# A hybrid SSD and attention layer: the fourth z block moved behind B, and a second step cut in slices

## The chip, the cores and the metric

The kernel runs on one core of a Trainium2 chip. The metric is the device time of one execution in microseconds (us), as the median of several executions. Before the change it is 838.3 us (three runs, 838.29 to 838.42).

## The reference

One layer over 256 tokens of width 2048, in float32. The input is normalised, goes through one wide projection whose columns belong to two groups, a state-space (SSD) scan and a causal attention without softmax, and both results go through an output projection:

```python
h = rmsnorm(x, norm_w)
proj = h @ w_in
z, xbc, dt_raw, q, k, v, g = jnp.split(proj, IN_SPLITS, axis=-1)
xbc = silu(causal_depthwise_conv(xbc, conv_w, conv_b))      # -> xs (2048), B (512), C (512)
y = ssd_chunked_scan(xs, softplus(dt_raw + dt_bias), -exp(a_log), bm, cm) + d_skip * xs
yg = y * silu(z);  y_ssd = group_rmsnorm(yg) * ssd_norm_w   # four groups of 512
y_sba = stick_breaking_attention(q, k, v) * silu(g)         # 16 heads of 128
out = rmsnorm(x + concat(y_ssd, y_sba) @ w_out, final_norm_w)
```

w_in is 2048 x 13344 and w_out 4096 x 2048; reading them is most of the traffic, and multiplying with them is most of the work.

## The kernel before

**Blocks and steps.** The projections are a list of blocks (L922 to L953), each of some columns of a weight. The blocks of z (z0 to z3, 512 columns), c1 (C's second half and dt), v and o have the kind "tok": the tokens are the rows of the result. Those of c0, b, x, q, k and g have the kind "feat", with 256 columns: the features are the rows. Order before: z0 to z3, c0, c1, b0, b1, the first half of q0, x0_0 to x3_1, the second half of q0, k0, v0, g0, then q, k, v, g of the attention groups 1 to 3, then o0 to o3. A block of z has 8 steps, each of two slices of 128 rows of the weight, and a block of "feat" has 4 steps of four slices.

**One step.** `load` (L192) fetches two steps' weights at once into one of four buffers (raw) by SyncE's queue. `cut` (L207) splits a step's weights into hi, a rounded copy by ScalarE (L222), and lo, the rest by VectorE (L225); activations are split in the same way (hT_hi, hT_lo). `product` (L240) then multiplies: for "tok" three matmuls of 512 columns for each slice and half of the tokens (L253 to L255), 12 in a step; for "feat" matmuls of 512 (L259) and of 256 columns (L262), 16 in a step. The cuts run two steps ahead of the products (`ahead=2`).

**The first block.** In z0, `run_blocks` (L279) writes the order out by hand. For each step s: `turn_x` (L387) transposes two slices of x on TensorE, `scale_x` (L398) scales each by norm_w and splits it (ScalarE, then VectorE), and `advance` calls `cut`. In step 0 this goes slice by slice, `scale_x` and then half of the cut; in the steps from 1 on both `scale_x` come first and then one cut over both slices. z0 also loads x, in eight parts between its weights (L200).

**The rows' scale.** hT is at first x * norm_w without the norm's factor 1/rms per token. z0 to z3 are multiplied with that, and the factor r_tok is applied when the result is taken out of PSUM (`fin_z`, L441, L445: a SiLU with `scale=r_tok`). `square_x`, `row_scale` and `row_scale_bc` work the factor out during z1. `scale_h` (L427), eight calls of one ScalarE and three VectorE operations, then multiplies hT by it in place: slice pair i after step i + 2 of z3, the last two in c0 (L924). All later blocks use the scaled hT.

**Side work.** Everything between the blocks (convolutions, the scan, the attention) sits in queues as small functions with a cost for VectorE and one for ScalarE. After each step `drain` (L145) takes functions from the queues, in the order of the queues, until a budget, 1.5 and 1.6 for most blocks, is used; a rest below zero is carried on. `lag` keeps a queue closed for so many steps after a function, `when` waits for a condition. `drain_all` (L166) empties all queues; `fin_proj` calls it at the end of g0 (L763), and then gives the scan's memory (pool ssd) to the attention's tiles.

**The scan.** After each x block `conv` (L465) runs; after a group's second block `ssd_group` (L620) queues: `back` (transposes and two VectorE operations of 512 columns for each half), `state_in` (L661, one VectorE operation), `decay` (eight exps, L654), `state` (L666, the product `ps_st`), `mat`, `yoff`, `yout` (L682, the products `ps_y`, then the gate with sz, L690, and squares), `scale` (a chain of small VectorE operations), `rescale` (L704) and `mix` twice (L708: transposes `ps_ms`, then L716 on ScalarE and L717 on VectorE). The small results in PSUM (`side_ps`, L70) share four buffers; a block's accumulators have their own two.

**The attention.** For each of a group's four heads `scores` (L780: `ps_z`, three sigmoids, four masks on GpSimd, a scan and products on VectorE), `weights_T` (L803: transposes `ps_w`) and `attend` (L813) are queued, staggered over the heads.

**The order on the engines.** Outside z0 it is not the written order: when the program is built, a planner with modelled durations places each instruction on its engine by its place in the program, with the cuts ahead, and lets later ones go first where an earlier one isn't ready by the model. The exps of group 0's `decay`, for instance, are called in x2 and run from 154.9 us on, in q0_0. On the chip each engine keeps to the order so made.

Of the kernel before, what the change touches and what calls it, by code (L numbers as in the profile page):

```python
# [12 lines left out]
AF = mybir.ActivationFunctionType  # L13
# [9 lines left out]
KIN = D_MODEL // P  # L23
# [29 lines left out]
def hybrid_kernel(ctx, tc, x, norm_w, w_in, conv_w, conv_b, dt_bias, a_log, d_skip,  # L53
                  ssd_norm_w, w_out, final_norm_w, out):
    nc = tc.nc
    ve, ac, te, gp = nc.vector, nc.scalar, nc.tensor, nc.gpsimd
# [13 lines left out]
    def side_ps(name):  # L70
        return ps_s.tile([P, 512], F32, tag="s", name=name)
# [70 lines left out]
    def push(q, cost, fn, lag=0, when=None):  # L142
        q.items.append((cost, lag, fn, when))
# [32 lines left out]
    def block(name, w, c0, n, nk, acts, kind, finish, budget, start=None, pool=None, trail=0):  # L176
        blocks.append(dict(name=name, w=w, c0=c0, n=n, nk=nk, acts=acts, kind=kind, finish=finish, budget=budget,
                           start=start, pool=pool, trail=trail))

    def chunks():  # L180
        for b in blocks:
            for kc in range(b["nk"] // KC[b["kind"]]):
                yield b, kc

    def steps():
        for b in blocks:
            for s in range(b["nk"] // KS[b["kind"]]):
                yield b, s

    raws, cuts, last_cut, after = {}, {}, [None], {}  # L190
# [88 lines left out]
    def run_blocks(ahead=2):  # L279
        todo_load, todo_cut = chunks(), steps()  # L280
        lead = {"load": 0, "cut": 0}
        done = 0

        def advance_load(want):
            while lead["load"] < want:
                c = next(todo_load, None)
                if c is None:
                    break
                load(*c)
                lead["load"] += 1  # L290

        def advance(n_cut, each=None):
            while lead["cut"] < n_cut:
                nxt = next(todo_cut, None)
                if nxt is None:
                    return
                b, s = nxt
                advance_load(lead["cut"] // 2 + 4)
                if s == 0 and b["start"] is not None:
                    b["start"]()  # L300
                with (tc.high_priority() if b is not blocks[0] else ExitStack()):
                    cut(b, s, each)
                lead["cut"] += 1


        with tc.manual_schedule(engines={te.engine, ac.engine, ve.engine}):
            b = blocks[0]
            acc = new_acc(b)
            advance_load(2)

            ac.copy(ysq[:, 0, 0:1], ones[:, 0:1])
            warm = side_ps("warm")

            def warm_up(n):
                for i in range(n):
                    te.matmul(warm[:, 0:P], lhsT=ident, rhs=ident, start=True, stop=True)
            warm_up(5)
            load_rows(nwT, nw_rows, KIN, "ps_nw")
            turn_x(0)
            warm_up(2)  # L320
            advance(1, each=scale_x)
            product(b, 0, acc, range(NB), (0,))
            for s in range(1, KIN // 2 + 1):
                if s < KIN // 2:
                    turn_x(s)
                    for i in range(2):
                        scale_x(2 * s + i)
                    advance(s + 1)
                product(b, s - 1, acc, range(NB), (1,) if s == 1 else None)
                done += 1  # L330
            load_params()
        b["finish"](acc)

        for b in blocks[1:]:
            name, trail = b["name"], b["trail"]
            ns = b["nk"] // KS[b["kind"]]
            acc = new_acc(b)
            for s in range(ns + trail):
                advance(done + 1 + ahead)
                if trail == 0:  # L340
                    product(b, s, acc, range(2))
                else:
                    if s < ns:
                        product(b, s, acc, (0,))
                        if s == ns - 1:
                            b["finish"](acc, 0)
                    if s == ns + trail - 1:
                        halves = [ps_mm.tile([P, 2, 512], F32, tag="mm", name=f"mm_{name}_1_{h}")[:, 0, :]
                                  for h in range(2)]
                        product_end(b, s - trail, 1, halves)  # L350
                    elif s >= trail:
                        product(b, s - trail, acc, (1,))
                if s < ns:
                    done += 1
                if (name, s) in after:
                    after[name, s]()
                drain(b["budget"])
            if trail == 0:
                b["finish"](acc)
            else:  # L360
                b["finish"]([acc[1]] + halves, 1)

    r_tok = const.tile([P, NB], F32, name="r_tok")
# [23 lines left out]
    def turn_x(s):  # L387

        q, h = divmod(s, 2)
        for j in range(2):  # L390
            k = 2 * s + j
            pt = side_ps(f"ps_x_{k}")
            for b in range(NB):
                te.transpose(out=pt[:, b * P:(b + 1) * P],
                             in_=xt[q][:, b, h * 256 + j * P:h * 256 + (j + 1) * P], identity=ident)
            xT[k] = pt[:, 0:SEQ]

    def scale_x(k):  # L398
        ac.activation(hT_hi[:, k, :], xT[k], AF.Copy, scale=nwT[:, k:k + 1])
        ve.scalar_tensor_tensor(out=hT_lo[:, k, :], in0=xT[k], scalar=nwT[:, k:k + 1],  # L400
                                in1=hT_hi[:, k, :].bitcast(F32), op0=ALU.mult, op1=ALU.subtract)
# [25 lines left out]
    def scale_h(s):  # L427

        ks = slice(2 * s, 2 * s + 2)
        hi, lo = hT_hi[:, ks, :], hT_lo[:, ks, :]  # L430
        t = ssd.tile([P, 2, SEQ], F32, tag="tmp", name=f"h_{s}", bufs=2)
        ve.tensor_tensor(out=t, in0=hi.bitcast(F32), in1=lo.bitcast(F32), op=ALU.add)
        ve.tensor_tensor(out=t, in0=t, in1=r_bc.unsqueeze(1).broadcast_to([P, 2, SEQ]), op=ALU.mult)
        ac.copy(hi, t)
        ve.tensor_tensor(out=lo, in0=t, in1=hi.bitcast(F32), op=ALU.subtract)


    sz = [mixp.tile([P, NB, GW], F32, tag="mix1", name=f"sz_{g}", bufs=4) for g in range(GROUPS)]
    main = queue()

    def fin_z(i):  # L441
        def f(acc):
            def evac():
                for t in range(NB):
                    ac.activation(sz[i][:, t, :], acc[t], AF.Silu, scale=r_tok[:, t:t + 1])  # L445
            if i > 0:
                evac()
                return
            for q in range(KIN // 4):
                for b in range(NB):  # L450
                    push(main, (0, 0.7), lambda q=q, b=b: square_x(q, b))
            push(main, (1.0, 0), row_scale, lag=1)
            push(main, (0.6, 0.7), row_scale_bc)
            push(main, (0, 1.1), evac, lag=8)
            push(main, (0.5, 0), turn_params)
        return f
# [142 lines left out]
    norm_q, scan_q, conv_q = queue(), queue(), queue()  # L599
    turned, summed, scanned, segs = set(), set(), set(), {}  # L600
# [19 lines left out]
    def ssd_group(g, w):  # L620
# [103 lines left out]
        if g == 0:  # L724
            push(scan_q, (0, 0), lambda: seg(0), when=lambda: g in turned)
            push(scan_q, (0, 0), lambda: seg(1), lag=3)
        push(scan_q, (0.6, 0), state_in, lag=1, when=lambda: g in turned)
        push(scan_q, (0, 2.4), lambda: decay(0))
        push(scan_q, (0, 0.6), state)
        push(scan_q, (1.2, 0), lambda: mat(0), lag=1)  # L730
# [188 lines left out]
            return mix_hi[k // 4][:, k % 4, :], mix_lo[k // 4][:, k % 4, :]  # L919
        return mix_a["hi"][:, k - KIN, :], mix_a["lo"][:, k - KIN, :]  # L920

    for i in range(4):  # L922
        block(f"z{i}", w_in, Z0 + i * 512, 512, KIN, h_acts, "tok", fin_z(i), (1.5, 1.6))
    for i in range(8):  # L924
        after[*(("z3", i + 2) if i < 6 else ("c0", i - 6))] = lambda i=i: scale_h(i)
    block("c0", w_in, C0, 256, KIN, h_acts, "feat", fin_c0, (1.5, 1.6))
    block("c1", w_in, C0 + 256, 256 + HEADS, KIN, h_acts, "tok", fin_c1, (0.7, 0.8))
    for h in range(2):
# [5 lines left out]
    def block_att(which, grp, halves=range(2)):  # L934
        c0 = {"q": Q0, "k": K0, "v": V0, "g": G0}[which] + grp * 512
        if which == "v":
            block(f"v{grp}", w_in, c0, 512, KIN, h_acts, "tok", fin_proj("v", grp), (1.5, 1.6))
            return
        for h in halves:
            block(f"{which}{grp}_{h}", w_in, c0 + h * 256, 256, KIN, h_acts, "feat", fin_proj(which, grp, h), (1.5, 1.6))  # L940


    block_att("q", 0, (0,))
    for g in range(GROUPS):
        block_x(g)
    block_att("q", 0, (1,))
    for grp in range(4):
        for which in "qkvg" if grp else "kvg":
            block_att(which, grp)
    for i in range(4):  # L950
        block(f"o{i}", w_out, i * 512, 512, 2 * KIN, m_acts, "tok", fin_last if i == 3 else fin_out(i), (1.5, 1.6),
# [32 lines left out]
```

## Time and profile before

| | |
|---|---|
| median of the runs | 838.3 us |
| profiled execution, its own time | 837.85 us |
| its span, from first to last instruction | 836.1 us |
| TensorE (PE) busy | 821.3 us, 98% |
| weight loads of TensorE (PEld), beside the matmuls | 701.2 us, 84% |
| VectorE (DVE) busy | 519.7 us, 62% |
| ScalarE (ACT) busy | 446.3 us, 53% |
| GpSimd (POOL) busy | 61.8 us, 7% |

The blocks lie in the span about like this: z0 from 6 to 33 us, z1 to 55, z2 to 77, z3 to 99, c0 and c1 to 123, b to 147, q0_0 to 158, x to 261, q0_1 to 276, k0 to 301, v0 to 327, g0 to 357, then the attention's groups 1 to 3 to about 650, and o to the end. A busy TensorE is not one at its peak, since the ends of matmuls are modelled and overlap the next one's start; from one start to the next a matmul of 512 columns takes about 0.23 us here.

### The profile page before, as it was taken

How to read it: one execution, taken by the hardware profiler on the slowest of the kernel's cores; microseconds unless marked ns; L12 is line 12 of the kernel's file. 1: busy time of each engine (PE TensorE's matmuls, PEld its weight loads, DVE VectorE, ACT ScalarE, POOL GpSimd, SP SyncE). 2: the span in 40 equal slices, each digit the busy share in tenths (PEclk: the TensorE clock that was granted, in tenths of full speed). 3: DMA queues.
4: the chain of work that ended last, by engine and by line, in shares of the span. 5: the costliest groups of instructions: out<-in, count | busy, mean ns of one | idle time of the engine just before them, and what ended most of it. 6: DMA issues, size and time to landing. Idle time of an engine off the chain costs nothing.

```text
span 836.1 us, 11189 instructions
## 1 busy us (share of the span) xinstructions
PE 821.3 (98%) x4345; PEld 701.2 (84%) x4345; DVE 519.7 (62%) x713; ACT 446.3 (53%) x670; POOL 61.8 (7%) x125
## 2 busy tenths in 40 slices
PE   8999999999999999999999999999999999999995
PEld 7888898888887888888888888888888888888884
DVE  5655968578798867667445754466545755455543
ACT  5754558865685747464444544455444444344433
POOL 0000000100100101013000400022000310000000
PEclk9999999999999999999999999999999999999999
DMA  9855476665556555554466546654565845555712
GB/s 311 280 180 192 136 231 201 207 197 169 190 160 211 172 182 177 151 151 152 153 201 201 152 150 201 196 165 150 194 184 179 343 151 186 184 188 198 252 51 102
DMA packets 114410, 155.29 MB, mean 186 GB/s; under 512 B 3212, under 2 KB 79140, under 8 KB 113972
## 3 DMA queue, kind: packets, MB, share of 16 engines
q1 hardware_dynamic: 112996, 149.29, 56.1%
q0 software_dynamic: 1328, 5.28, 1.7%
q8 instruction: 34, 0.56, 0.3%
q14 instruction: 20, 0.16, 0.1%
q10 hardware_dynamic: 32, 0.01, 0.0%
HBM read 152.43 MB, written 2.13 MB: 185 GB/s over the span
## 4 chain that ended last, share of the span: by engine, by line
PE 92%; DVE 3%; ACT 2%; issue 1%; POOL 0%; ACTq 0%; POOLq 0%
PE mm_k L259 7%; PE mm_g L259 7%; PE mm_x L259 7%; PE mm_o L254 7%; PE mm_o L253 7%; PE mm_o L255 7%; PE mm_q L259 5%; PE mm_k L262 4%; PE mm_g L262 4%; PE mm_z L254 4%; PE mm_v L253 3%; PE mm_v L255 3%; PE mm_v L254 3%; PE mm_z L253 3%; PE mm_x L262 3%; PE mm_z L255 3%
## 5 line engine op out<-in xcount | busy, mean ns | idle before, releaser
L225 DVE TENSOR_TENSOR lo_o<-raw_o,hi_o 128x1024 fp32r<-128x1024 f32 x64 | 78.1, 1224 | 74.1 <-ACT hi_o L222 74.1
L222 ACT CAST hi_o<-raw_o 128x1024 fp32r<-128x1024 f32 x64 | 67.1, 1053 | 93.5 <-PE mm_o L255 79.9
L259 PE MATMUL mm_q<-hT,hi_q 128*128 128x512 f32 x256 | 82.7, 402 | 0.0
L259 PE MATMUL mm_x<-hT,hi_x 128*128 128x512 f32 x256 | 81.8, 401 | 0.0
L259 PE MATMUL mm_k<-hT,hi_k 128*128 128x512 f32 x256 | 81.5, 400 | 0.0
L259 PE MATMUL mm_g<-hT,hi_g 128*128 128x512 f32 x256 | 81.0, 398 | 0.0
L225 DVE TENSOR_TENSOR lo_v<-raw_v,hi_v 128x1024 fp32r<-128x1024 f32 x32 | 39.2, 1224 | 41.4 <-ACT hi_v L222 41.4
L225 DVE TENSOR_TENSOR lo_g<-raw_g,hi_g 128x1024 fp32r<-128x1024 f32 x32 | 39.2, 1224 | 40.4 <-ACT hi_g L222 39.5
L222 ACT CAST hi_v<-raw_v 128x1024 fp32r<-128x1024 f32 x32 | 33.7, 1052 | 50.7 <-PE mm_v L255 31.6
L262 PEld LDWEIGHTS mm_k<-hT,lo_k 128*128 128x128 f32 x256 | 48.1, 188 | 11.4
L262 PEld LDWEIGHTS mm_x<-hT,lo_x 128*128 128x128 f32 x256 | 48.1, 188 | 11.4
L262 PEld LDWEIGHTS mm_g<-hT,lo_g 128*128 128x128 f32 x256 | 48.1, 188 | 11.3
L262 PEld LDWEIGHTS mm_q<-hT,lo_q 128*128 128x128 f32 x256 | 48.1, 188 | 11.2
L225 DVE TENSOR_TENSOR lo_q<-raw_q,hi_q 128x1024 fp32r<-128x1024 f32 x32 | 39.2, 1225 | 29.1 <-ACT hi_q L222 24.7
L222 ACT CAST hi_g<-raw_g 128x1024 fp32r<-128x1024 f32 x32 | 33.6, 1050 | 42.8 <-PE mm_g L259 27.8
L222 ACT CAST hi_q<-raw_q 128x1024 fp32r<-128x1024 f32 x32 | 33.5, 1048 | 42.3 <-PE mm_q L259 17.0
L225 DVE TENSOR_TENSOR lo_k<-raw_k,hi_k 128x1024 fp32r<-128x1024 f32 x32 | 39.2, 1226 | 24.7 <-ACT hi_k L222 23.7
L225 DVE TENSOR_TENSOR lo_z<-raw_z,hi_z 128x1024 fp32r<-128x1024 f32 (+1 forms) x33 | 39.2, 1191 | 22.8 <-ACT hi_z L222 22.7
L225 DVE TENSOR_TENSOR lo_x<-raw_x,hi_x 128x1024 fp32r<-128x1024 f32 x32 | 39.2, 1225 | 19.7 <-ACT hi_x L222 18.0
L253 PE MATMUL mm_z<-hi_z,hT 128*128 128x512 f32 x128 | 51.1, 399 | 0.0
L254 PE MATMUL mm_z<-lo_z,hT 128*128 128x512 f32 x128 | 50.2, 392 | 0.8 <-DVE lo_z L225 0.8
L262 PE MATMUL mm_q<-hT,lo_q 128*128 128x256 f32 x256 | 50.6, 279 | 0.0
(250 smaller groups left out, 1977.6 us busy)
## 6 DMA issues: line engine op xcount, KB each, us to landing
raw_o<-in_w_out_dram SPq DMA_DIRECT2D x32, 1024.0 KB, 5.2
raw_q<-in_w_in_dram SPq DMA_DIRECT2D x16, 1024.0 KB, 5.3
raw_x<-in_w_in_dram SPq DMA_DIRECT2D x16, 1024.0 KB, 5.4
raw_k<-in_w_in_dram SPq DMA_DIRECT2D x16, 1024.0 KB, 5.3
raw_v<-in_w_in_dram SPq DMA_DIRECT2D x16, 1024.0 KB, 5.0
raw_g<-in_w_in_dram SPq DMA_DIRECT2D x16, 1024.0 KB, 5.3
raw_z<-in_w_in_dram SPq DMA_DIRECT2D x12, 1024.0 KB, 5.0
raw_b<-in_w_in_dram SPq DMA_DIRECT2D x4, 1024.0 KB, 5.4
```

What stands on the lines that cost most here:

```text
L222: ins = ac.copy(hi[:, ks, :], src[:, ks, :])
L225: ve.tensor_tensor(out=lo[:, ks, :], in0=src[:, ks, :], in1=hi[:, ks, :].bitcast(F32), op=ALU.subtract)
L253: te.matmul(o, lhsT=ah[:, ts], rhs=hi[:, k2, :], start=first, stop=False)
L254: te.matmul(o, lhsT=ah[:, ts], rhs=lo[:, k2, :], start=False, stop=False)
L255: te.matmul(o, lhsT=al[:, ts], rhs=hi[:, k2, :], start=False, stop=last)
L259: te.matmul(acc[i], lhsT=hi[:, k2, i * P:(i + 1) * P], rhs=hT[:, k, :, :].rearrange("p a s -> p (a s)"), start=first, stop=False, skip_gro ...
L262: te.matmul(acc[i][:, 0:SEQ], lhsT=lo[:, k2, i * P:(i + 1) * P], rhs=hT_hi[:, k, :], start=False, stop=last, skip_group_check=True)
```

## The change

- In z0's step 1 the activations and weights are prepared slice by slice, as in step 0: `scale_x`, half of the cut, `scale_x`, the other half.
- The block z3 moves from behind z2 to behind b1. The first half of q0, which stood there, moves behind x3_1, so that q0 is now whole, right before k0.
- `scale_h` follows the steps of z2 instead of z3. So z3 is multiplied with the scaled hT, and its evacuation has no `scale=r_tok`.
- `state_in` gets a lag of 2 steps instead of 1.

```diff
             for s in range(1, KIN // 2 + 1):
-                if s < KIN // 2:
+                if s == 1:
+                    turn_x(s)
+                    advance(s + 1, each=lambda i: scale_x(2 + i))
+                elif s < KIN // 2:
                     turn_x(s)
                     for i in range(2):
                         scale_x(2 * s + i)
...
                 for t in range(NB):
-                    ac.activation(sz[i][:, t, :], acc[t], AF.Silu, scale=r_tok[:, t:t + 1])
+                    if i < 3:
+                        ac.activation(sz[i][:, t, :], acc[t], AF.Silu, scale=r_tok[:, t:t + 1])
+                    else:
+                        ac.activation(sz[i][:, t, :], acc[t], AF.Silu)
...
-        push(scan_q, (0.6, 0), state_in, lag=1, when=lambda: g in turned)
+        push(scan_q, (0.6, 0), state_in, lag=2, when=lambda: g in turned)
...
-    for i in range(4):
+    def block_z(i):
         block(f"z{i}", w_in, Z0 + i * 512, 512, KIN, h_acts, "tok", fin_z(i), (1.5, 1.6))
+
+    for i in range(3):
+        block_z(i)
     for i in range(8):
-        after[*(("z3", i + 2) if i < 6 else ("c0", i - 6))] = lambda i=i: scale_h(i)
+        after[*(("z2", i + 2) if i < 6 else ("c0", i - 6))] = lambda i=i: scale_h(i)
...
-    block_att("q", 0, (0,))
+    block_z(3)
     for g in range(GROUPS):
         block_x(g)
-    block_att("q", 0, (1,))
     for grp in range(4):
-        for which in "qkvg" if grp else "kvg":
+        for which in "qkvg":
             block_att(which, grp)
```

## Rows read from the trace of the kernel before

**Rows 1.** The page, busy us, share of the span and instructions of TensorE

```profile
PE 821.3 (98%) x4345; PEld 701.2 (84%) x4345; DVE 519.7 (62%) x713; ACT 446.3 (53%) x670; POOL 61.8 (7%) x125
```

**Rows 2.** What TensorE waited for: us in total, times, longest

```profile
PE ps_st L668 <- DVE mix_s_lo L717: 1.2, 1, 1.2
PE ps_w L808 <- PE mm_q L259: 0.8, 1, 0.8
...
PE ps_ms L714 <- ACT y L704: 0.5, 1, 0.5
PE ps_w L808 <- ACT sg L792: 0.5, 1, 0.5
PE ps_bt L541 <- ACT BT L475: 0.4, 1, 0.4
```

**Rows 3.** Stretches: length, busy us by engine (count), granted clock, DMA share, GB/s

```profile
77.40:99.20 21.80, 21.80 (x97) 18.04 (x97) 19.58 (x26) 13.22 (x17) 0.00 (x0) 1.00 0.49 150
...
158.30:172.40 14.10, 13.71 (x88) 12.05 (x87) 9.10 (x8) 12.62 (x30) 0.00 (x0) 1.00 0.49 150
```

**Rows 4.** Timeline, TensorE in z0: start, us, engine, line, out<-in, count, [idle before]

```profile
10.20 0.47 PE L253 MATMUL mm_z<-hi_z,hT 128*128 128x512 f32 x1
11.43 0.50 PE L254 MATMUL mm_z<-lo_z,hT 128*128 128x512 f32 x1 [0.76 <-DVE lo_z L225]
...
12.00 0.39 PE L253 MATMUL mm_z<-hi_z,hT 128*128 128x512 f32 x1
12.23 0.40 PE L254 MATMUL mm_z<-lo_z,hT 128*128 128x512 f32 x1
```

**Rows 5.** Timeline, ScalarE and VectorE in z0's first two steps

```profile
4.90 0.47 ACT L399 ACTIVATE hT<-ps_x,nwT 128x256 fp32r<-128x256 f32 x1 [2.12 <-PE ps_x L394]
...
5.91 0.69 DVE L225 TENSOR_TENSOR lo_z<-raw_z,hi_z 128x512 fp32r<-128x512 f32 x1
...
6.92 0.68 DVE L225 TENSOR_TENSOR lo_z<-raw_z,hi_z 128x512 fp32r<-128x512 f32 x1
...
8.35 0.84 ACT L399 ACTIVATE hT<-ps_x,nwT 128x256 fp32r<-128x256 f32 x2 [1.58 <-PE ps_x L394]
```

**Rows 6.** Loads of x: the issue of step 3's, and all eight to landing

```profile
4.29 0.89 SPq L383 DMA_DIRECT2D xt<-in_x_dram  x1
...
DMA to landing us min/median/max: 3.3/7.8/8.5
```

**Rows 7.** Timeline, from the scan's last products to the attention's first

```profile
355.08 1.90 PE L686 MATMUL ps_y<-xdt,seg 128*128 128x64 f32 x16
...
368.64 0.09 POOL L788 MEMSET kp<- 128x1 f32 x1 [45.61 <-ACT mix_s_hi L716]
...
369.20 0.46 PE L784 MATMUL ps_z<-k,q 128*128 128x128 f32 x2
...
369.94 0.39 PE L784 MATMUL ps_z<-k,q 128*128 128x128 f32 x2
```

**Rows 8.** Timeline, TensorE: the first two scores of attention group 1

```profile
458.50 0.38 PE L784 MATMUL ps_z<-k,q 128*128 128x128 f32 x2
...
464.73 0.39 PE L784 MATMUL ps_z<-k,q 128*128 128x128 f32 x2
```

**Rows 9.** ScalarE: z's evacuations (ns min/median/max), a table load and its successor

```profile
L445 ACT ACTIVATE sz<-mm_z,r_tok x8: 676/682/692, 43.7 to 101.0; 128x512 f32<-128x512 f32 x8
...
156.24 1.28 ACT L475 ACT_TABLE_LOAD   x1
157.53 0.42 ACT L475 ACTIVATE BT<-cacc 128x256 f32<-128x256 f32 x1
```

**Rows 10.** Timeline around the state product of scan group 1

```profile
252.36 0.60 PE L714 MATMUL ps_ms<-ident,y 128*128 128x128 f32 x4
...
253.61 0.87 DVE L717 SCALAR_TENSOR_TENSOR mix_s_lo<-ps_ms,snT,mix_s_hi 128x256 fp32r<-128x256 f32 x2
...
254.14 0.70 PE L668 MATMUL ps_st<-xds,Btok 128*128 128x512 f32 x1 [1.18 <-DVE mix_s_lo L717]
```

## The prediction

> **What bounds the kernel now.** I read the page first: TensorE is busy for 98% of the span [rows 1], and in the list of what it waited for the few waits add up to little [rows 2]. So the kernel is one row of matmuls, in an order that is fixed when the program is built, and time can come only out of the places where that row stands still. The stretches say the same: TensorE works through all 21.8 us of z3 although VectorE is busy for 19.58 of them, and the granted clock is 1.00, which is the 2.4 GHz level [rows 3]. Next I looked up where each wait lies.
>
> An idle time in the list is counted from the modelled end of the matmul before, and that is too little. In the first block a matmul starts 0.23 us after the last one (12.00, 12.23), and the one that waits starts 1.23 us after its forerunner (10.20, 11.43): 1.00 us are lost where 0.76 us are listed as idle [rows 4]. I add 0.2 us to every other wait for that.
>
> Of the waits, four matter here: 1.0 us in z0's second step [rows 4], 1.2 + 0.2 for `ps_st` (group 1's state product) [rows 2], and three at the start of the attention, 0.5, 0.8 and 0.5 us, with the additions 2.4 us [rows 2]. Together that is 4.8 us. A fifth, `ps_bt`, 0.4 + 0.2 us [rows 2], lies where z3 is to go.
>
> **The change, part by part.**
>
> *z0's second step in slices.* Before, ScalarE does both `scale_x` from 8.35 on, then one cast of 1024 columns, then VectorE one subtraction, and TensorE's second matmul stands until 11.43 [rows 4, 5]. The first step shows what the slices cost, since it is prepared that way already: from the start of its first `scale_x` (4.90) to the end of its first `lo` slice (5.91 + 0.69) it takes 1.70 us, to the end of the second (6.92 + 0.68) 2.70 us [rows 5]. From 8.35 on that gives 10.05 and 11.05. TensorE wants the first `lo` at 10.20 + 0.23 = 10.43 and the second six matmuls later, at 11.8. Both are there; 1.0 us is gone. The two smaller casts and subtractions are additions to ScalarE and VectorE of a few tenths of a us, hidden where ScalarE stands idle for 1.58 us before 8.35 [rows 5] and VectorE waits for it. What is late next: step 3 then turns x at about 10.20 + 12 x 0.23 = 12.96. Its x was issued at 4.29, and no load of x took over 8.5 us [rows 6], so it is there by 12.8 at the latest. Value 1.0 us, bounds 0.7 to 1.1.
>
> *`scale_h` after z2 instead of z3.* It needs r_bc. Walking `drain` by its budget (1.5, 1.6 a step), z1's steps 0 to 3 take the eight squares and `row_scale`, step 4 `row_scale_bc`; z2's step 2 comes later by far. The work is that which z3 carried without one wait of TensorE [rows 3], and c0 follows it as before. Only `turn_params` joins it, in z2's step 4: a few transposes and two short copies. The cover is the lead of the cuts, two steps of 12 x 0.23 = 2.8 us. Value 0, at worst 0.3.
>
> *z3 between b1 and x0, q0 whole after x.* The matmuls are the same ones, so the row is as long as before, and each raw load is of the same size. z3 has 8 steps where q0's half had 4; the x blocks come four steps later and have four more steps (32 instead of 28) from x3's end to the `drain_all` at g0's end. That is the part that counts. Walking the queues, the last `yout` of group 3 is taken in g0_1's last step in the old order, right before `drain_all`, and in g0_1's first step in the new, 3 x 2.8 = 8.3 us earlier; `scale` goes ahead of the `drain_all` too. The trace shows the old case: the last `ps_y` runs from 355.08 to 356.98, and only at 368.64, 11.7 us later, do the first tiles of the attention get the memory of the phase before (memset of kp) [rows 7]. By its place the first `scores` would come one step after 356.98 (2.8 us) and the second three steps after (8.3 us); both are held up and run together, at 369.20 and 369.94 [rows 7], and GpSimd, VectorE and ScalarE can't follow: the three waits. In group 1 the two are 6.2 us apart, at 458.50 and 464.73 [rows 8], and no such wait is listed there, each of the three being a single one [rows 2]. In the new order the memory comes free 11.7 - 8.3 = 3.4 us after the step's end, 0.6 us after the first `scores` is due and 5 us before the second. So the two `ps_w` waits go (1.7 us). That for `ps_ms`, 0.7 us, came because the chain to `y` was longer than planned for; the chain is the same, so I let 0.4 us of it stay. Value 2.4 - 0.4 = 2.0 us, bounds 0 and 2.4.
>
> The `ps_bt` wait: `conv` of b2 and b3 falls in z3's step 0 and `b_tok` in its step 3, just as in q0_0 before. It stays; value 0, bounds a gain of 0.6 and a loss of 0.3 (a step of z3 is a little shorter than one of q0).
>
> *z3's evacuation.* Two activations of 0.68 us [rows 9] move to the start of x0, where ScalarE is at its fullest, 12.62 of 14.1 us [rows 3], and where group 0's exps, planned far ahead of their place, are under way. A Silu between exps means two more table loads of 1.28 us [rows 9]. 2 x 1.28 + 1.36 = 3.9 us, against 1.5 us of free time in that stretch and a lead of the cuts of up to 5.6 us: value 0, at worst 1 us. After a load the next activation starts at once (156.24 + 1.28, then 157.53) [rows 9]. The Trainium skill (ScalarE: Activation LUTs, What ACT_TABLE_LOAD costs) puts a drain of 1.38 us beside each load, 2.66 us in all. The row contradicts the drain; by the page's figure the burst would be 2.8 us longer, and the forecast would be about 836.
>
> *`state_in` with lag 2.* `ps_st` waits until 254.14 for `mix_s_lo`, begun at 253.61; right before it, at 252.36, the second pair of mixes ran [rows 10]. There are four side tiles in PSUM; the mixes hold all four, the state product is the fifth, and `mix0.1` and `state1` were in one drain step. In the new walk `state1` is taken a whole step before `mix0.0`. The 1.4 us go; other pairs meet instead (`mix0.1`, then `yoff1` a step later; `mix1.1`, then `state2` a step later). For new waits of this sort I set 0.4 us; bounds 0 and 1.4, as large as the one shown.
>
> **The sum.** 1.0 + 1.4 + 2.0 - 0.4 = 4.0 us. The profiled execution took 837.85 us (span 836.1 and 1.75 around it), 0.45 less than the median of 838.3; the new one would take 833.8, the median 834.3.
>
> **The rivals.**
> A. The planned waits only change places: the attention still begins in a bunch (group 3's last work is again planned into the end of g0), and the scan finds another wait like that of `ps_st`. Then the slices alone are left: 838.3 - 1.0 = 837.3. For it: all the waits but the first come from an order planned by modelled times, and everything after b1 is planned anew. Against it: group 1 to 3 show that an attention that begins on time has no such wait.
> B. Slower: VectorE falls behind in the scan, and the fifth side tile waits for `mix_s_lo` in all four groups, 4 x 1.4 instead of 1 x 1.4 = 4.2 us more; group 3 is then late too and the bunch stays. 838.3 - 1.0 + 4.2 = 841.5. It decides where VectorE is over one step (2.8 us) behind when a pair of mixes ends. For it: the new walk puts two `back` (each two operations of 0.68 us), `state_in`, `scale` and a `conv` into three successive steps. Against it: the mixes come three steps after these.
> C. ScalarE's burst at z3's evacuation comes with four more loads instead of two: 4 x 1.28 + 1.36 = 6.5 us, less 1.5 us free and one step of lead, 2.8 us, where the other is used up, is 2.2 us of waiting; 836.5 at the sum above, 837.2 where `ps_bt` waits longer by its bound as well and half of the new waits doubles. The page's drain would make it likelier; the row speaks against it.
>
> **How the numbers follow.** A measurement of this kernel can tell about 0.2%, 1.7 us, from no change. The forecast, 834.3, has 0.75, with its own range from 832.2 (all bounds of gain: 1.0 + 1.4 + 2.4 + 0.6, and 0.7 for the small waits that are left) to 836.3. A has 0.14, C 0.04 and B 0.07. The range to 837.4 takes in A and C and leaves out B. Faster 0.75, same 0.18, slower 0.07.
>
> **What would show it.** Right: no wait for `lo_z` at 11.4 us; `ps_z` of the first two scores about 6 us apart and no `ps_w` wait of over 0.3 us; kp's first memset about 3.4 us after g0's last step; no `ps_st` wait. Wrong: two `ps_z` within 1 us of each other (A); waits of side products for `mix_s_lo` in several groups (B); waits of mm_x for `hi_x` at about 170 us, between table loads (C). The prediction fails as a whole if the row of matmuls itself gets longer, which would show in a start-to-start time other than 0.23 us.

## The result, and the profile after

The changed kernel takes 833.69 us (median of six runs, 833.11 to 833.83), against 838.29 us of the kernel before beside it. The ratio is 0.9943 with a 95% interval of 0.993 to 0.9956: faster by 0.57%, 4.6 us by the medians. Its profiled execution took 833.74 us, 4.1 us less than the profiled one of before (837.85), and the lines below are of that one.

The page first, and the list of what TensorE waited for, complete:

```profile
span 832.0 us, 11195 instructions
PE 820.6 (99%) x4345; PEld 701.0 (84%) x4345; DVE 522.0 (63%) x714; ACT 449.0 (54%) x673; POOL 60.9 (7%) x125
```

```profile
PE warm L316 <- POOL ident masks.py:199: 1.5, 1, 1.5
PE ps_bt L547 <- ACT BT L481: 0.7, 1, 0.7
PE ps_ac L581 <- DVE da L513: 0.2, 1, 0.2
```

TensorE does the same 4345 matmuls in nearly the same busy time [rows 1]; what went are the places where it stood. Of the five waits of [rows 2] only `ps_bt` is left, and it has grown from 0.4 to 0.7 us. The lines have moved by up to six: L541 of before is L547 here, L717 is L723.

The start of z0's second step, in the order of time (columns as in [rows 4]):

```profile
8.07 0.42 PEld L397 LDWEIGHTS ps_x<-ident,xt 128*128 128x128 f32 x4 [0.42 <-DMA xt<-in_x_dram]
...
9.45 0.62 ACT L222 CAST hi_z<-raw_z 128x512 fp32r<-128x512 f32 x1 [0.43 <-DMA raw_z<-in_w_in_dram]
...
10.11 0.69 DVE L225 TENSOR_TENSOR lo_z<-raw_z,hi_z 128x512 fp32r<-128x512 f32 x1 [0.56 <-ACT hi_z L222]
...
10.16 0.42 PEld L397 LDWEIGHTS ps_x<-ident,xt 128*128 128x128 f32 x4 [0.47 <-DMA xt<-in_x_dram]
...
10.58 0.47 PE L253 MATMUL mm_z<-hi_z,hT 128*128 128x512 f32 x1
10.89 0.46 PE L254 MATMUL mm_z<-lo_z,hT 128*128 128x512 f32 x1
```

The matmul that started 1.23 us after its forerunner [rows 4] now starts 0.31 us after it. But the block z1 starts at 32.42 here and at 33.00 before, 0.58 us earlier and not 1.0: two loads of x came late in this execution, and the transposes waited for them (at 8.07 and 10.16). The weights' load was late too (ScalarE waits 0.43 us for it), but `lo` is done at 10.80, before the matmul at 10.89 wants it.

Scan group 1 and the start of the attention, TensorE's side products alone and the first memset of kp:

```profile
237.70 1.02 PE L674 MATMUL ps_st<-xds,Btok 128*128 128x512 f32 x2
241.34 0.60 PE L720 MATMUL ps_ms<-ident,y 128*128 128x128 f32 x4
...
344.97 1.90 PE L692 MATMUL ps_y<-xdt,seg 128*128 128x64 f32 x16
355.12 1.04 PE L720 MATMUL ps_ms<-ident,y 128*128 128x128 f32 x8
358.80 0.38 PE L790 MATMUL ps_z<-k,q 128*128 128x128 f32 x2
...
365.02 0.39 PE L790 MATMUL ps_z<-k,q 128*128 128x128 f32 x2
```

```profile
356.38 0.09 POOL L794 MEMSET kp<- 128x1 f32 x1 [45.82 <-PE ps_ms L720]
```

The state product runs ahead of the mixes, where before it stood behind them [rows 10]. The last `ps_y` is ten microseconds earlier than in [rows 7], the scan's memory comes free at 356.38 instead of 368.64, and the first two scores are 6.2 us apart, like those of group 1 [rows 8], and not 0.74.

### The profile page after: what moved, and what is told of

It reads as the page before. It is cut to its first block, busy times and chain, and to the rows that moved or that the text cites. A ratio compares the mean times of both kernels' runs of the same rounds, so it can differ in the third digit from the quotient of the medians.

```text
span 832.0 us, 11195 instructions
## 1 busy us (share of the span) xinstructions
PE 820.6 (99%) x4345; PEld 701.0 (84%) x4345; DVE 522.0 (63%) x714; ACT 449.0 (54%) x673; POOL 60.9 (7%) x125
## 4 chain that ended last, share of the span: by engine, by line
PE 94%; DVE 2%; ACT 2%; issue 1%; POOL 0%; ACTq 0%; POOLq 0%
PE mm_x L259 7%; PE mm_k L259 7%; PE mm_g L259 7%; PE mm_o L255 7%; PE mm_o L254 7%; PE mm_o L253 7%; PE mm_q L259 7%; PE mm_k L262 4%; PE mm_x L262 4%; PE mm_g L262 4%; PE mm_v L253 4%; PE mm_v L255 3%; PE mm_v L254 3%; PE mm_q L262 3%; PE mm_z L254 3%; PE mm_z L253 3%
## 5 line engine op out<-in xcount | busy, mean ns | idle before, releaser
L222 ACT CAST hi_k<-raw_k 128x1024 fp32r<-128x1024 f32 x32 | 33.6, 1050 | 32.3 <-PE mm_k L259 24.9
L262 PE MATMUL mm_k<-hT,lo_k 128*128 128x256 f32 x256 | 50.4, 278 | 0.0
```

Source lines behind the costliest of these rows:

```text
L222: ins = ac.copy(hi[:, ks, :], src[:, ks, :])
L262: te.matmul(acc[i][:, 0:SEQ], lhsT=lo[:, k2, i * P:(i + 1) * P], rhs=hT_hi[:, k, :], start=False, stop=last, skip_group_check=True)
```

## The experiments

Times are medians beside runs of the kernel before on the same chip, 837.9 to 838.3 us; the ratio to it and its interval stand behind them. "Start to start" is what a matmul's start is later than the usual distance, as in the prediction.

**One part alone.** First the three parts of the change, one by one, and the change without its lag.

```diff
+                if s == 1:                                  # e1_slices: only this
+                    turn_x(s)
+                    advance(s + 1, each=lambda i: scale_x(2 + i))
+                elif s < KIN // 2:
...
-        push(scan_q, (0.6, 0), state_in, lag=1, when=...)   # e2_lag: only this
+        push(scan_q, (0.6, 0), state_in, lag=2, when=...)
```

> The kernel before with the sliced second step alone. Theory: the waits of TensorE are independent terms, and slicing removes the one at 11.4 us: 1.00 us less by start-to-start times, so 837.3 against 838.3; up to 0.4 us of it can be eaten by the loads of x and of z0's weights, which landed later in the profile of the changed kernel (there z1 starts only 0.58 us earlier): 837.3 to 837.7. All waits from 40 us on stay as they were, shifted. Rival: the prologue is bound by the loads and not by the order of the slices; then z1 starts within 0.2 us of before.

Measured: 837.21 us, 0.999 (0.9981 to 0.9999). In its profile z1 starts at 31.91, 1.09 us earlier than before; the list of waits then shows what took part of it back:

```profile
PE ps_st L671 <- DVE mix_s_lo L720: 1.2, 1, 1.2
PE ps_w L811 <- PE mm_q L259: 0.9, 1, 0.9
PE ps_bt L544 <- ACT BT L478: 0.8, 1, 0.8
```

In this execution the prologue is not bound by its loads. In the changed kernel's profile the two late loads of x did cost something: the matmuls behind them start at 8.49 and 10.58, where they start at 8.28 and 10.12 here. The `ps_bt` wait grew (start to start from 0.55 to 0.92 us), so of 1.09 us the span kept 0.6. That the other waits stay as they were holds for `ps_st` and the attention, not for this one.

> The kernel before with lag 2 of state_in alone. Theory: the wait of ps_st (1.34 us by start-to-start times) came from the fifth side tile, since mix0.1 and state1 were in one drain step; it goes. But with the old order of blocks the walk of the queues puts the last yout of group 3 behind the drain_all, so that the scan's memory comes free later than 368.6 us and the attention begins in a larger bunch: 2.75 us of waits there become 3.5 to 6. Time 837.8 to 840. Rival: the lag alone gives its 1.3 us and changes nothing else, 837.0; or VectorE's backlog is the cause and the wait comes back at another side product of group 1, 838.3.

Measured: 836.9 us, 0.9983 (0.9975 to 0.9992). The `ps_st` wait is gone from the list, and nothing came in its place. The rest of the theory missed: the waits at the attention are the same 2.7 us to a few hundredths, though by the walk of the queues the last yout falls behind the `drain_all`. In the trace the last `ps_y` stands where it stood, at g0's end (353.66). So the place in the queue alone doesn't make the bunch.

> The changed kernel without slices and with lag 1: the order of the blocks and the place of scale_h alone. Theory: the three waits at the attention's start go (2.75 to 0.4 us), that of ps_bt grows by 0.27, that of ps_st stays at about 1.3, since with lag 1 the walk puts mix0.1 and state1 into one drain step again: 838.3 - 2.3 + 0.3 = 836.3. Rival: without lag 2 the bunch at the attention stays: 838 or more.

Measured, the changed kernel with those two edits undone: 834.63 us, 0.996 (0.9946 to 0.9973). It beat its expectation, 836.3, because the `ps_st` wait didn't stay. The rows show how near it is:

```profile
241.45 0.60 PE L717 MATMUL ps_ms<-ident,y 128*128 128x128 f32 x4
242.03 1.12 PE L671 MATMUL ps_st<-xds,Btok 128*128 128x512 f32 x2
```

```profile
241.49 0.87 DVE L720 SCALAR_TENSOR_TENSOR mix_s_lo<-ps_ms,snT,mix_s_hi 128x256 fp32r<-128x256 f32 x2
```

`ps_st` still starts as the first of the two `mix_s_lo` operations ends (two of 0.48 us, from 241.49), but TensorE hardly reaches it earlier: its mixes end then as well, and 0.14 us are lost. The bunch at the attention is gone.

> The changed kernel with lag 1 alone undone. Theory: the ps_st wait of group 1 is back, 1.3 us: 833.7 + 1.3 = 835.0, and the attention still begins with its scores about 6 us apart. Rival: in the new order the lag is worth nothing (833.7), or more than the one wait, because the bunch at the attention comes back too (837 or more).

Measured: 833.93 us, 0.9951 (0.9939 to 0.9964); that can't be told from the whole change, and the 835.0 of its theory did not come. In the profile the wait is there with 0.3 us idle, 0.48 start to start, and again ends with the first `mix_s_lo` (240.91 + 0.48, `ps_st` at 241.44):

```profile
241.44 1.12 PE L674 MATMUL ps_st<-xds,Btok 128*128 128x512 f32 x2 [0.32 <-DVE mix_s_lo L723]
```

So the parts don't add up. Alone they take 0.6, 1.4 and 3.3 us off the span of 836.1 us, 5.3 together; the whole change takes 4.1. The `ps_st` wait, 1.34 us, is counted twice in that sum, once for the lag and once for the order.

**Is it a buffer that `ps_st` waits for?** In the kernel before, with lag 1, the two slices of a mix share one side tile, so that a pair of mixes holds two of the four buffers. The diff shows two kernels; the second (e10) has both parts.

```diff
-                pt = side_ps(f"ps_ms_{g}_{j}")              # e7_mix_one_bank, in mix
+                if i == 0:
+                    pm = side_ps(f"ps_ms_{g}_{j2}")
+                pt = pm[:, i * SEQ:(i + 1) * SEQ]
...
+            for i in range(2):                              # e10_mix_turn_first: all transposes,
+                ...                                         # then hi and lo of both slices
```

> The kernel before with the two slices of a mix in one side tile (two halves of 256 columns) instead of two tiles, lag 1. Theory: ps_st waited for the buffer of the first mix, as the fifth side tile; with two tiles for the four slices it needs none of theirs, the 1.34 us go and ps_st runs before the first mix_s_lo is done: 838.0 - 1.3 = 836.7. The attention's waits stay at 2.7 or get a little longer, as transposes of two slices now share a tile. Rival: VectorE's backlog makes the wait, not the buffers; it stays at 1 us or more.

Measured: 840.46 us, 1.0025 (1.0016 to 1.0034): slower. `ps_st` no longer waits, but its neighbour does, since the second slice's transposes now write a tile that the first slice's `lo` still reads; at the attention one wait of 2.2 us stands in place of two.

```profile
254.55 0.44 PE L716 MATMUL ps_ms<-ident,y 128*128 128x128 f32 x2 [1.97 <-DVE mix_s_lo L719]
...
255.16 1.02 PE L668 MATMUL ps_st<-xds,Btok 128*128 128x512 f32 x2
```

That kernel added a dependency of its own and settles nothing on the buffers, so the transposes were put first:

> The kernel before with the two slices of a mix in one side tile, and all their transposes ahead of the operations that read them (in the run with one tile a slice's transposes stood behind the other's reads, 2.1 us). Theory: ps_st waited for a buffer of the mixes, as the fifth side tile; now a pair of mixes holds two of four. The wait of 1.34 us goes: 838.0 - 1.3 = 836.7, with the waits at the attention at 2 to 2.7 as before. Rival: it stays or moves to another side product, since VectorE's backlog of that stretch makes it whatever the buffers are: 838.0.

Measured: 835.92 us, 0.9974 (0.9964 to 0.9984). `ps_st` starts at 252.77, right behind the mixes and 0.8 us before the first `mix_s_lo` even begins:

```profile
252.33 0.60 PE L713 MATMUL ps_ms<-ident,y 128*128 128x128 f32 x4
252.77 1.02 PE L668 MATMUL ps_st<-xds,Btok 128*128 128x512 f32 x2
```

```profile
253.58 0.48 DVE L720 SCALAR_TENSOR_TENSOR mix_s_lo<-ps_ms,snT,mix_s_hi 128x256 fp32r<-128x256 f32 x1
```

VectorE is as late as before; it was the buffer that passed its lateness on. Of the 1.9 us by which the profiled span is shorter (834.2 against 836.1), 1.3 are this, and most of the rest is a slightly smaller bunch at the attention (2.3 us).

**What makes the bunch at the attention?** Next the place of q0, with z3 where it was before. The diff shows two kernels, each with one of the two new lines:

```diff
-    block_att("q", 0, (0,))
+    block_att("q", 0)                # e6_q0_ahead: whole, here
     for g in range(GROUPS):
         block_x(g)
-    block_att("q", 0, (1,))
+    block_att("q", 0)                # e5_q0_behind: whole, here instead
```

> The kernel before with its first half of q0 moved behind x3_1, and nothing else: z3 stays behind z2, lag 1, no slices. Theory: what the new order gives at the attention comes from the 32 steps between x3 and the drain_all, not from z3 between B and x. The walk of the queues is that of the new order with lag 1 (last yout in g0_0's last step); so ps_ms and both ps_w waits go, the two first scores stand about 6 us apart, and the time is that of the order alone, 835 (838.0 - 3). Rival: z3 in that place matters by itself, as cover for the convolutions of B; then x0 starts with waits for b_tok and the cb products of 1 us or more, and the time is over 836.

Measured: 835.44 us, 0.9963 (0.9949 to 0.9977). The bunch is gone, with z3 still behind z2: the last `ps_y` starts at 345.71, the scores at 362.33 and 368.56. Two other things stand in the profile: `ps_st` waits its full 1.2 us, and there is a new wait for the transposes of the first `back` (0.6 us). Here x0 follows b1 directly, where before the first half of q0 and in the changed kernel z3 stands between; so a block in that place seems to be some cover for the first x group. Its profiled execution also lost 1.4 us in z0 (below), so its span can't be compared.

> The kernel before with both halves of q0 ahead of x0_0, so 24 steps instead of 28 lie between x3 and the drain_all. Theory: the walk puts mat, decay, yoff and both yout of group 3 behind the drain_all; the scan's memory comes free 15 to 20 us after g0's last step instead of 11.7, three scores run in a bunch, and TensorE waits 4 to 8 us there instead of 2.7: 839.5 to 843.5. Rival: the waits at the attention come from its first scores as such (table load, cold queues) and not from when the memory comes free: 838, unchanged.

Measured: 837.43 us, 0.9992 (0.9983 to 1.0001). This can't be told from no change, there is no larger bunch, and with that the theory that counted steps fell. Both yout run together at the end of g0. The memory does come free late, 17.2 us after g0's last step (351.0 to 368.23; before 13.6, from 355.08 to 368.64). But again only two scores run together, and TensorE's waits there add up to some 2.3 us, not 4 to 8. The kernel gives the scores' tiles two buffers each, which would keep a third score out; no run tests that. The exps and `mat` of group 3, which the walk had put behind the `drain_all`, the planner had run by 340 us. The `ps_st` wait is smaller here too, 0.14 us in group 1 and 0.47 in group 2 instead of 1.34.

```profile
353.98 3.68 PE L686 MATMUL ps_y<-xdt,seg 128*128 128x64 f32 x32
...
368.79 0.47 PE L784 MATMUL ps_z<-k,q 128*128 128x128 f32 x2
...
369.53 0.38 PE L784 MATMUL ps_z<-k,q 128*128 128x128 f32 x2
```

With 24 steps, with 28 and with a lag of 2 the last `ps_y` stands at g0's end, and two scores run in a bunch; with 32 it stands 10 to 13 us earlier, and there is none. So the place of the last `ps_y` should be the cause, and holding back that alone in the changed kernel should bring the bunch back:

```diff
+        if g == GROUPS - 1:
+            push(scan_q, (0, 0), lambda: None, lag=3)
         push(scan_q, (1.2, 0.7), lambda: yout(1))
```

> The changed kernel, with the last yout of group 3 held back by three steps, to g0's last step, where it stood before the change; the blocks keep their new order. Theory, as the runs with 24, 28 and 32 steps left it: the bunch at the attention's start depends on where the last ps_y stands against g0's last step, since its chain of about 11 us to the last transposes frees the memory. So the waits of ps_ms and ps_w come back, 2.75 us instead of 0.45, and the first two scores stand under 1 us apart: 833.7 + 2.3 = 836.0. Rival: the new order brings its gain in another way (four steps more for the whole scan, less load on VectorE); then at most 0.5 us are lost.

Measured: 836.56 us, 0.9978 (0.9968 to 0.9987), against 0.9943 for the change. The waits are back with nearly their old sizes (start to start 0.58, 1.01, 0.66 and two of 0.19):

```profile
PE ps_w L816 <- PE mm_q L259: 0.8, 1, 0.8
PE ps_w L816 <- ACT sg L800: 0.5, 1, 0.5
...
PE ps_ms L720 <- ACT y L710: 0.4, 1, 0.4
```

```profile
354.47 1.90 PE L692 MATMUL ps_y<-xdt,seg 128*128 128x64 f32 x16
...
368.47 0.46 PE L792 MATMUL ps_z<-k,q 128*128 128x128 f32 x2
```

The last `ps_y` stands at g0's end again, 9.5 us later than in the changed kernel, the first scores are later with it, and the second ones follow 0.73 us behind, as before. From v0's first matmul to v1's TensorE takes 105.91 us, 2.25 more than in the changed kernel (103.66), close to the 2.3 expected; the medians differ by 2.9.

**The wait that is left.** `ps_bt` needs the SiLU of b3's convolution. ScalarE in the changed kernel, from the exps' table load on:

```profile
129.87 1.28 ACT L660 ACT_TABLE_LOAD   x1
132.54 0.40 ACT L660 ACTIVATE seg<-seg,nacs 128x128 f32<-128x128 f32 x1 [1.38 <-POOL seg L652]
132.85 1.04 ACT L222 CAST hi_z<-raw_z 128x1024 fp32r<-128x1024 f32 x1
133.91 1.28 ACT L481 ACT_TABLE_LOAD   x1
135.20 0.42 ACT L481 ACTIVATE BT<-cacc 128x256 f32<-128x256 f32 x1
```

It loads the exps' table, stands 1.38 us for a seg, does one exp, loads the table of the SiLU, and is then late. The seg comes through memory:

```profile
131.42 1.09 POOL L652 TENSOR_SCALAR_AFFINE_SELECT seg<-seg 128x1024 f32<-128x1024 f32 x1 [5.10 <-DMA seg<-acT_d]
```

The same exp stands ahead of that SiLU in the kernel before and in the one with slices alone, where it waits 0.37 us longer, as much as the wait for `ps_bt` grew there:

```profile
154.88 0.40 ACT L654 ACTIVATE seg<-seg,nacs 128x128 f32<-128x128 f32 x1 [1.55 <-POOL seg L646]
```

```profile
154.21 0.40 ACT L657 ACTIVATE seg<-seg,nacs 128x128 f32<-128x128 f32 x1 [1.92 <-POOL seg L649]
```

Two kernels go at that from either side: `b_tok` two steps later, and the exps' source later.

```diff
-                push(main, (1.2, 0.8), lambda g=g: conv(ut[:, g, :], BN + g, BT[:, g, :]), lag=g // 3 * 3)
+                push(main, (1.2, 0.8), lambda g=g: conv(ut[:, g, :], BN + g, BT[:, g, :]), lag=g // 3 * 5)   # e8_btok_later
...
             if h == 0:                                # e11_decays_out_later
-                push(main, (0.4, 0), decays_out)
                 return
+            push(main, (0.4, 0), decays_out)
```

> The changed kernel with b_tok two steps later (lag 5 instead of 3 after conv of b3). Theory: the ps_bt wait, 0.8 us there, comes because ScalarE stands behind an exp of group 0 whose seg is still on its way from memory, with the SiLU of b3 behind it; two steps later, 5.5 us, that is done, nothing else needs Btok or cb before x1: 833.7 - 0.8 = 832.9. Rival: the cb products or the x convolutions behind it are now late, or the wait moves to another product; then no gain.

Measured: 832.83 us, 0.9932 (0.992 to 0.9945). No wait for `ps_bt` is left, and behind z0 no other came.

> The changed kernel with decays_out (whose write to memory feeds the first seg and so the first exps of the scan) queued behind the convolutions of b2 and b3. Theory: the ps_bt wait, 0.8 us, is ScalarE standing behind an exp whose seg is still on its way; with the exps later the SiLU of b3 goes ahead, the wait is gone, and the two table loads around it too: 832.9, as with b_tok later. Rival: the SiLU of b3 is late by itself (VectorE's convolution): the wait stays at 0.5 or more and the time at 833.5.

Measured: 832.7 us, 0.9938 (0.9926 to 0.9951). The exps' load comes at 141.0, the two SiLU run at 130.78 and 133.44, the second 1.8 us before the transposes at 135.23, and `ps_bt` is off the list:

```profile
130.78 0.41 ACT L481 ACTIVATE BT<-cacc 128x256 f32<-128x256 f32 x1
132.49 1.05 ACT L222 CAST hi_z<-raw_z 128x1024 fp32r<-128x1024 f32 x1 [1.31 <-PE mm_z L255]
133.44 0.41 ACT L481 ACTIVATE BT<-cacc 128x256 f32<-128x256 f32 x1
```

The convolution was in time; the exp ahead of its SiLU, with its own wait and the two table loads around it, was the cause. Both kernels are about 0.9 us faster than the change by the medians, but their intervals overlap with its own; the profiles, with the wait listed or not, are the firmer ground.

**The slices once more,** with the wait out of the way that had eaten part of them: the kernel with the later `b_tok`, its second step in one piece as before the change.

> The kernel with b_tok two steps later, without the slices in z0's second step. Theory: where no later wait takes back what the prologue gains, the slices are worth the whole wait at 11.4 us, 1.0 to 1.1 us: 832.8 + 1.05 = 833.9. Rival: they are worth 0.3 to 0.7, as the runs with and without them so far gave (0.7 between the order alone and the order with slices).

Measured: 834.06 us, 0.9948 (0.9935 to 0.996), 1.2 us more than with the slices (832.83). The intervals overlap, and this kernel's profiled execution, itself at the median, began more slowly than most (last section): its z1 starts at 33.61 us. So the size is rough; the sign agrees with the start of z1, 31.89 to 32.42 us in the five profiles with slices that began alike, and 33.00 to 33.09 in five without.

## Why the prediction was right

834.3 us was forecast, 833.69 came. The profiled execution was forecast at 833.8 and took 833.74; the 0.45 us added for the median did not come again. By terms, in us start to start, forecast and measured in the profile:

| step | forecast | measured |
|---|---|---|
| slices in z0 | -1.0 (0.7 to 1.1) | -0.58 here; 1.09 with slices alone |
| `scale_h` beside z2 | 0 | 0 |
| the attention's waits | -2.0 (0 to 2.4) | -2.3 (2.75 to 0.45) |
| `ps_bt` | 0 (-0.6 to +0.3) | +0.27 |
| z3's evacuation | 0 (to +1) | 0 |
| `ps_st`, and new waits of its kind | -1.4 + 0.4 | -1.34 + 0 |
| sum | -4.0 | -4.1 (span; the last 0.15 not traced) |

That the sum fits to 0.1 us is partly luck. The slices gave 0.4 us too little and `ps_bt` cost 0.27; the attention gave 0.3 us more, and the 0.4 us set for new waits were not used.

*The slices.* The mechanism held; the size in this one execution is below the bounds, because two loads were late that the prediction took to be there: it weighed only step 3's x, and it was the x of the two steps ahead of it that came late. Without that the 1.0 us are there (1.09 with slices alone).

*`scale_h`.* In the stretch of z2 VectorE is busy for 19.85 us, and TensorE for all of it, as in z3 before [rows 3]:

```profile
54.60:76.80 22.20, 22.20 (x99) 18.17 (x98) 19.85 (x27) 13.24 (x17) 0.00 (x0) 1.00 0.49 148
```

*The attention.* The step was right in its cause, that the last yout ahead of the `drain_all` holds up the memory, and the run with yout held back shows it. Two things in it were off. The number of steps between x3 and `drain_all` was taken for the lever; 24 steps and 28 both give a bunch, so it works only by moving the last `ps_y` off g0's end. And the memory was to come free 3.4 us after the step, by a chain of 11.7 us from the end of `ps_y`. It does so 1.3 us after (355.12 to 356.38), 9.5 us from the end of `ps_y`; with the order alone and with q0 behind x, where `ps_y` stands a step earlier, it is 1.3 us after the step as well, and 12.3 us from `ps_y`. So that chain no longer sets the time: the last mixes run at g0's end, by their own place. Nothing of the `ps_ms` wait stayed, where 0.4 us were left for it.

*`ps_bt`.* The bound was hit: TensorE comes to it 0.26 us sooner after `ps_acT` (13.91 instead of 14.17 us, first matmul to first matmul), since four steps of z3 are that much shorter (2.72 us each, against 2.79 for q0). The cause under it is ScalarE's early exp, which the prediction did not name for this wait.

*z3's evacuation.* The value 0 was right, but not the picture of it. Group 0's exps were to be under way there; they are over by 147 us, four microseconds before. And there were to be two more table loads; with the order alone there is none (17 in all, as before), since the load at the evacuation stands in place of the one that x's convolutions had at 179.5 us. The two more of the changed kernel (19) come with the lag, which has 19 alone too. In the 14.1 us from x0's start on ScalarE is busy for 8.21 us, not 12.62, and TensorE for all of it:

```profile
149.80:163.90 14.10, 14.10 (x82) 12.32 (x81) 6.74 (x7) 8.21 (x10) 0.00 (x0) 1.00 0.65 196
```

The evacuation's activations take 0.60 us and not 0.68, without the scale from memory:

```profile
151.08 1.28 ACT L451 ACT_TABLE_LOAD   x1
152.38 0.60 ACT L451 ACTIVATE sz<-mm_z 128x512 f32<-128x512 f32 x1
```

Rival C falls with that. The activation follows its load within 20 ns again, so the drain that the Trainium skill (ScalarE: Activation LUTs, What ACT_TABLE_LOAD costs) counts beside a load doesn't show here either.

*`ps_st`.* The buffer was the cause, as the mixes in half as many tiles showed. But the prediction credited all of it to the lag; in the new order it goes from 1.34 to 0.48 us (with slices) or 0.14 (without) even with the old lag, and the lag is worth 0.1 to 0.5 us there, which the times can't tell from nothing. The 0.4 us for new waits of that kind weren't needed, and of rival B nothing is seen. Rival A needed the bunch to stay and did not come.

*Two sums.* Rival C's 837.2 should be 837.0, if half of the 0.4 us of new waits doubles. And with the 2.8 us that the prediction adds there, the burst at z3's evacuation would be 6.7 us, still under the 1.5 and up to 5.6 us set against it; 836 follows only where part of that lead is used up.

## What to carry to other kernels

Where one engine is busy for 98% and more, list its waits with their places and ask of each what the waiting instruction needs and who holds that; here a buffer, a pool's memory and an in-order neighbour stood behind three of them. When parts of a change meet at the same wait, their gains don't add: undo each from the whole as well as trying each alone. An instruction planned far ahead of its place is not free on an in-order engine, since what stands behind it waits for its data: 0.8 us of TensorE's time here.

## What the runs showed of the hardware that was not expected

The first microseconds differ between executions of equal code. In most profiles z0's matmuls, where nothing holds them up, start 0.23 us apart from 7.0 us on; with q0 behind x and with yout held back they start 0.43 us apart until 10.7 us, and in two more (the mixes in one tile; the later `b_tok` without slices) until 7.6 and 8.0 us. Two of the timeline with yout held back:

```profile
7.25 0.63 PE L255 MATMUL mm_z<-hi_z,hT 128*128 128x512 f32 x1
7.68 0.63 PE L253 MATMUL mm_z<-hi_z,hT 128*128 128x512 f32 x1
```

The stretches' clock column says 1.00 for these microseconds too, but only because the trace has no record of the clock there, and the column counts such time as 1.00. The records begin, at the full 2.4 GHz, at 10.72 us with q0 behind x, at 10.64 with yout held back, at 7.51 and 7.93 in the two others, and between 5.0 and 6.7 us in the remaining ten profiles: in all four within 0.1 us of where the wider distances end. So TensorE seems to be at its lower level until then. The Trainium skill (TensorE: Matmul & The Clock Gate, Wait — 56ns, not 53.3ns?) gives 426.7 ns from start to start for 512 columns at the lower level, 1.2 GHz; the distances here are that. Block z1 starts at 34.42 us in the one, without slices, and at 33.72 in the other, with them: 1.3 to 1.8 us later than in the profiles above, which is more than the slices gain, so the prologue of a single profile is not to be compared without looking at these distances first.
